# Token columns sent to TensorE as even places, then odd places, and put back in order by the evacuations

## The chip, the cores and the metric

The kernel runs on one core of a Trainium2 chip, in one launch. The metric is the device time of that launch in microseconds, as the median of several runs; 1412.37 us before the change. The engines of the core are TensorE (PE, with its weight loads shown as PEld), VectorE (DVE), ScalarE (ACT), GpSimd (POOL) and SyncE (SP), each with a queue of its own.

## The reference

One inference step of a hybrid decoder layer (one layer, model width 2048) for 256 prompt tokens and 8 sample tokens, all in fp32. Cut to its core:

```python
xn = rms_norm(x, g_mix)
z  = xn @ w_in                       # 2048 -> 3584: pool u, lru x, lru gelu gate, conformer a and b
y_pool = (pool_mixer(u_pool) ...) @ w_pool_br          # 512 -> 2048
y_lru  = (rg_lru(causal_dwconv(u_lru)) * gelu(u_gel)) @ w_lru_br      # 1024 -> 2048
y_conf = silu(layer_norm(causal_dwconv(c_a * sigmoid(c_b)))) @ w_conf_br   # 512 -> 2048
g_a, g_b, g_c = split(sigmoid(xn @ w_gate + b_gate), 3)               # 2048 -> 3 x 2048
x = x + (g_a * y_pool + g_b * y_lru + g_c * y_conf) @ w_out
x = x + square(relu(rms_norm(x, g_mlp) @ w_up)) @ w_down              # 2048 -> 8192 -> 2048
y = rms_norm(x, g_final)             # and the new states of the three mixers
```

## The kernel before

All activations lie with channels on the 128 partitions and the 264 tokens (256 prompt, 8 sample) side by side in the free dimension, 1056 bytes of each partition per tile of 128 channels. A dense layer is then a row of matmuls whose stationary operand is a 128 x 128 block of weights and whose moving operand is one such tile with its 264 columns; the sum over the input channels grows in a PSUM bank (`acc`, eight of them, one 2 KiB bank each).

To keep fp32 precision at the speed of the rounded type `float32r`, weights and activations are each split into a high part (the rounded value) and a low part (the rest). A *split product* is three matmuls, high by high, high by low and low by high (`mm3`, L150 to L153). The very first four products are written out in another order with the same three terms (`first_mm`, L826).

The weights come from HBM in chunks of 128 x 1024, in an order laid down by `weight_plan`. A chunk holds 2 x 4 blocks, that is 8 split products or 24 matmuls. `split` (L147 and L148) rounds a chunk on ACT into `whi` and takes the rest on DVE into `wlo`; both rings have four places, and the split runs three chunks ahead of its use (`AHEAD`). Four banks are filled side by side by the chunks of one group: 8 chunks for a layer with 2048 input channels, 4 for `w_lru_br`, 2 for `w_pool_br` and `w_conf_br`.

After the last chunk of a group each of its four banks is read once, by an evacuation: `lru_x_copy`, `lru_x_evac`, `gel_evac`, `cb_evac`, `ca_evac`, `pool_evac` (the columns of `w_in`), `gate_evac` (L675), `branch_evac` (L688), `out_evac` (L714), `up_evac` (L748), `down_evac` (L764), all on DVE, and on ACT the sigmoids of the small block-diagonal products (`lru_gate_mm`, L404 and L405) and the scale of the pooling products (`grp_mm`, L650). Those that feed a convolution write the prompt columns and the eight sample columns apart. Three all-ones products for the norms (L222, L549, L907) take plain fp32 tiles and do not go through `mm3`.

The order of every engine's queue is written out by the program: work beside the dense stream (convolutions, scans, norms, splits of activations) stands in three queues (`stage`, `run_bg`) or is put off by so many chunks (`later`), with a budget for each engine and chunk. At about 435 us the last evacuations of the LRU branch (L688) are followed on POOL by four additions (L691) and two sums (L542, L543), after which an all-ones product of the conformer's norm (L549) stands in TensorE's queue. At the end, the last `down_evac` is followed by the final norm and the writing of y.

Of the kernel before, what the change touches and what calls it, by code (L numbers as in the profile page):

```python
# [11 lines left out]
AF = mybir.ActivationFunctionType  # L12
ALU = mybir.AluOpType
AX = mybir.AxisListType

P = 128
D = 2048
TP = 256
TS = 8
N = TP + TS  # L20
# [57 lines left out]
def hybrid_step(ctx: ExitStack, tc: tile.TileContext, x_in, par_in, st_in, wall, y_out, st_out):  # L78
    nc = tc.nc
# [4 lines left out]
    def f(ap):  # L84
        return ap.bitcast(F32)
# [7 lines left out]
    X = GX[:, KD:].rearrange("p (k n) -> p k n", k=KD)  # L93
# [6 lines left out]
    rstd = cpool.tile([P, N], F32, name="rstd")  # L100
# [5 lines left out]
    def pv(name, i=None, n=1):  # L106
        a, b = PCOL[name]
        return par[:, a:b] if i is None else par[:, a + i:a + i + n]
# [5 lines left out]
    pext = qtmp[:, 2900:2900 + 4 * (15 + TP)].rearrange("p (g n) -> p g n", g=4)  # L114
    vext = B[3].rearrange("p a n -> p (a n)")[:, 8 * N - 4 * (30 + TP):].rearrange("p (g n) -> p g n", g=4)
# [24 lines left out]
    def split(j, half=None):  # L140
# [6 lines left out]
        nc.scalar.copy(h[:, s], r[:, s])  # L147
        nc.vector.tensor_tensor(lo[:, s], r[:, s], f(h[:, s]), op=ALU.subtract)  # L148

    def mm3(ps, whi_t, wlo_t, xh, xl, first, last):  # L150
        nc.tensor.matmul(ps[:, :N], whi_t, xh, start=first, stop=False)  # L151
        nc.tensor.matmul(ps[:, :N], whi_t, xl, start=False, stop=False)  # L152
        nc.tensor.matmul(ps[:, :N], wlo_t, xh, start=False, stop=last)  # L153
# [47 lines left out]
    def spend(**kw):  # L201
        for e, c in kw.items():
            credit[e] -= c
# [48 lines left out]
    el = B[0].rearrange("p a n -> p (a n)")[:, :8 * (TP + 3)].rearrange("p (a n) -> p a n", a=8)  # L252
# [55 lines left out]
    st_lc = st[:, S_LC:S_LC + 256].rearrange("p (c b k) -> p c b k", c=8, b=8)  # L308
    st_cc = st[:, S_CC:S_CC + 992].rearrange("p (c b k) -> p c b k", c=4, b=8)
    st_po = st[:, S_POOL:S_POOL + 512].rearrange("p (c b k) -> p c b k", c=4, b=8)  # L310
# [3 lines left out]
    TM, GEL, RA, _ = B  # L314
# [10 lines left out]
        return slice(2 * c, 2 * c + 2)  # L325

    def lru_x_copy(ct, ps):
        nc.vector.tensor_copy(CT[:, ct, :], ps[:, :N])
        spend(dve=0.42)

    def lru_x_scale():
# [3 lines left out]
        lru_conv(range(4))  # L335

    def lru_x_evac(ct, ps):
        nc.vector.tensor_tensor(el[:, ct, 3:], ps[:, :TP], rstd[:, :TP], op=ALU.mult)
        nc.vector.tensor_tensor(st_lc[:, ct, :, 3], ps[:, TP:N], rstd[:, TP:], op=ALU.mult)
        spend(dve=0.5)  # L340

    def lru_conv(cts):
# [52 lines left out]
    def lru_gate_mm(ct, c, j):  # L395
        assert "xc" in done
        hi, lo = whi[:, c % NHI, :], wlo[:, c % NHI, :]
        out = []
        for t in range(2):
            s = slice((2 * j + t) * P, (2 * j + t + 1) * P)  # L400
            ps = acc()
            mm3(ps, hi[:, s], lo[:, s], L[:, ct, :], L[:, 8 + ct, :], True, True)
            out.append(ps)
        nc.scalar.activation(RA[:, ct, :], out[0][:, :N], AF.Sigmoid, bias=pv("b_lru_a", ct))  # L404
        nc.scalar.activation(TM[:, ct, :], out[1][:, :N], AF.Sigmoid, bias=pv("b_lru_x", ct))  # L405
        spend(act=1.0)
        if ct % 2:
            def times():
                nc.vector.tensor_tensor(XC[:, ct - 1:ct + 1, :], XC[:, ct - 1:ct + 1, :], TM[:, ct - 1:ct + 1, :],
                                        op=ALU.mult)  # L410
                spend(dve=0.71)

            later(1, times)
# [57 lines left out]

    def gel_evac(ct, ps):
        assert "conv" in done
        nc.vector.tensor_tensor(GEL[:, ct, :], ps[:, :N], rstd, op=ALU.mult)
        spend(dve=0.4)

    def gelu(c0):
# [16 lines left out]
    CT = G[:, 12:16, :]  # L494
    SG = G[:, 16:20, :]
    VC = G[:, 20:24, :]

    def cb_evac(ct, ps):
        nc.vector.tensor_tensor(SG[:, ct, :], ps[:, :N], rstd, op=ALU.mult)
        spend(dve=0.43)  # L500
        if ct == 3:
            later(1, lambda: nc.scalar.activation(SG, SG, AF.Sigmoid))
            later(2, scaled)
# [3 lines left out]
        spend(dve=1.25)  # L507

    def ca_evac(ct, ps):
        nc.vector.tensor_tensor(vext[:, ct, 30:], ps[:, :TP], SG[:, ct, :TP], op=ALU.mult)  # L510
        nc.vector.tensor_tensor(st_cc[:, ct, :, 30], ps[:, TP:N], SG[:, ct, TP:], op=ALU.mult)
        spend(dve=0.5)

    def conf():
# [79 lines left out]


    def pool_evac(gi, ps):
        nc.vector.tensor_tensor(pext[:, gi, 15:], ps[:, :TP], rstd[:, :TP], op=ALU.mult)
        nc.vector.tensor_tensor(st_po[:, gi, :, 15], ps[:, TP:N], rstd[:, TP:], op=ALU.mult)
        spend(dve=0.5)

    Sa = qtmp[:, 0:4 * W].rearrange("p (g n) -> p g n", g=4)
# [1 line left out]
    DU = G[:, 8:12, :]  # L603
# [39 lines left out]
    def grp_mm(c):  # L643
        assert "pool" in done
        hi, lo = whi[:, c % NHI, :], wlo[:, c % NHI, :]
        for gi in range(4):
            s = slice(gi * P, (gi + 1) * P)
            ps = acc()
            mm3(ps, hi[:, s], lo[:, s], Q(gi), Q(8 + gi), True, True)
            nc.scalar.activation(DU[:, gi, :], ps[:, :N], AF.Copy, scale=pv("pool_scale", gi))  # L650
        stage_split("pool", 2, lambda c: Q(slice(2 * c, 2 * c + 2)), lambda c: Q(slice(8 + 2 * c, 10 + 2 * c)), lambda c: DU[:, 2 * c:2 * c + 2, :])
        mark("pool", "grp")

# [18 lines left out]
    def gate_evac(br, g, m, ps):  # L672
        assert {"b_term", "grp"} <= done and (br != 1 or g % 2 == 0 or "lru" in done) and ("conf" in done or br < 2 or g < 3)
        t = gate_tile(br, g, m)
        nc.vector.tensor_tensor(t, ps[:, :N], rstd, op=ALU.mult)  # L675

        def rest():
            nc.scalar.activation(t, t, AF.Sigmoid, bias=pv("b_gate", br * 16 + g * 4 + m))
            spend(act=0.5)

        spend(dve=0.43)
        later(1 + m // 2, rest)

    def branch_evac(br, g, m, ps):
        assert "grp" in done and (br < 1 or "lru" in done) and (br < 2 or "conf" in done)
        t = gate_tile(br, g, m)
        k = g * 4 + m
        nc.vector.tensor_tensor(t, ps[:, :N], t, op=ALU.mult)  # L688
        spend(dve=0.43)
        if br == 1:  # L690
            nc.gpsimd.tensor_tensor(partial(k), t, gate_tile(0, g, m), op=ALU.add)  # L691
            spend(pool=0.8)
        if br == 2:
            nc.gpsimd.tensor_tensor(t, t, partial(k), op=ALU.add)
            spend(pool=0.8)
            later_split(A[:, k, :], A[:, 16 + k, :], t, 1)
# [14 lines left out]
    sq2 = G[:, 20, :]  # L711

    def out_evac(m, ps):
        nc.vector.tensor_tensor(X[:, m, :], X[:, m, :], ps[:, :N], op=ALU.add)  # L714
        spend(dve=0.4)

        hi, lo = bpart(m)

        def one():
            nc.scalar.activation(hi, X[:, m, :], AF.Copy, scale=pv("g_mlp", m))  # L720
            square_add(m)
            spend(act=0.8)

        def other():
            nc.vector.scalar_tensor_tensor(lo, X[:, m, :], pv("g_mlp", m), f(hi),
                                           op0=ALU.mult, op1=ALU.subtract)
            spend(dve=0.35)

        later(m % 4 // 2, one)
        later(m % 4 // 2 + 1, other)  # L730
        if m == KD - 1:
            later(4, lambda: rms_close(sq2))
# [12 lines left out]
    def up_evac(q, m, ps):  # L745
        hi, lo = hid(q, m)
        t = G[:, m % 8, :]
        nc.vector.scalar_tensor_tensor(t, ps[:, :N], 0.0, rstd, op0=ALU.max, op1=ALU.mult)  # L748
        spend(dve=0.4)

        def one():
            nc.scalar.activation(t, t, AF.Square)
            nc.scalar.copy(hi, t)
            spend(act=0.8)

        def other():
            nc.vector.tensor_tensor(lo, t, f(hi), op=ALU.subtract)
            spend(dve=0.35)

        later(1 + m % 4 // 2, one)  # L760
        later(2 + m % 4 // 2, other)

    def down_evac(q, m, ps):
        nc.vector.tensor_tensor(X[:, m, :], X[:, m, :], ps[:, :N], op=ALU.add)  # L764
        spend(dve=0.4)
        if q == 3:
            def rest():
                square_add(m, m < KD - 2)
                nc.scalar.activation(X[:, m, :], X[:, m, :], AF.Copy, scale=gfin[:, m:m + 1])

            later(0 if m >= KD - 4 else 1 + m % 4 // 2, rest)
# [50 lines left out]
    def first_mm(rhs, pss):  # L822
        xh, xl = rhs(0)
        for w, x, start in ((whi, xh, True), (whi, xl, False), (wlo, xh, False)):
            for m in range(4):
                nc.tensor.matmul(pss[m][:, :N], w[:, 0, m * P:(m + 1) * P], x, start=start, stop=False)  # L826

    def tile_mm(i, c, kt, m, rhs, pss, stop):
        s = slice(kt * 512 + m * P, kt * 512 + (m + 1) * P)
# [16 lines left out]
    pss = None  # L846
    for i, ch in enumerate(chunks):
# [13 lines left out]
        kind, gi, c, _ = ch  # L861
        if kind == "dense":
            rhs, fn = group(gi)
            n = groups[gi][2] // 2
            if c == 0:
                pss = [acc() for _ in range(4)]
# [38 lines left out]
    ps = acc()  # L905
# [3 lines left out]
    t = G[:, 9, :]  # L909
# [104 lines left out]
```

## Time and profile before

| what | value |
|---|---|
| median of 3 runs | 1412.37 us (1411.13 to 1413.04) |
| span of the profiled execution, first to last instruction | 1410.3 us |
| granted TensorE clock over the span | 0.997 |
| busy: PE, PEld | 1396.0 us, 1394.3 us (99%) |
| busy: DVE, ACT, POOL | 830.4, 718.7, 98.0 us (59%, 51%, 7%) |
| DMA | 256.95 MB, mean 182 GB/s |

The page gives the profiled execution's own time as its span alone; what the metric counts around the span is the difference to the runs. Busy time of PE counts a matmul from its start to its modelled end, several at once being in flight, so the mean of one (285 ns) is longer than the distance from one to the next. Rows of groups read: line, engine, operation, output<-inputs, shape, count, then busy time and mean of one, then the idle time before them and what ended it.

### The profile page before, as it was taken

How to read it: one execution, taken by the hardware profiler on the slowest of the kernel's cores; microseconds unless marked ns; L12 is line 12 of the kernel's file. 1: busy time of each engine (PE TensorE's matmuls, PEld its weight loads, DVE VectorE, ACT ScalarE, POOL GpSimd, SP SyncE). 2: the span in 40 equal slices, each digit the busy share in tenths (PEclk: the TensorE clock that was granted, in tenths of full speed). 3: DMA queues.
4: the chain of work that ended last, by engine and by line, in shares of the span. 5: the costliest groups of instructions: out<-in, count | busy, mean ns of one | idle time of the engine just before them, and what ended most of it. 6: DMA issues, size and time to landing. Idle time of an engine off the chain costs nothing.

```text
span 1410.3 us, 26593 instructions
## 1 busy us (share of the span) xinstructions
PE 1396.0 (99%) x11418; PEld 1394.3 (99%) x11418; DVE 830.4 (59%) x1031; ACT 718.7 (51%) x1005; POOL 98.0 (7%) x122
## 2 busy tenths in 40 slices
PE   9999999999999999999999999999999999999996
PEld 9999999999999999999999999999999999999996
DVE  7685787776766648565545445544455544455443
ACT  7657576656664645454544334543344533354543
POOL 0230010110102103010000000000000000000012
PEclk9999999999999999999999999999999999999998
DMA  9455555555655554555555555555555555555551
GB/s 335 161 187 187 167 199 183 179 181 181 211 179 177 176 182 153 207 181 179 181 180 180 182 183 181 182 183 180 182 181 182 184 181 181 180 180 180 180 180 62
DMA packets 39286, 256.95 MB, mean 182 GB/s; under 512 B 4352, under 2 KB 5760, under 8 KB 9728
## 3 DMA queue, kind: packets, MB, share of 16 engines
q1 hardware_dynamic: 37872, 253.12, 52.9%
q8 instruction: 89, 1.46, 0.4%
q10 hardware_dynamic: 1152, 1.09, 0.2%
q0 software_dynamic: 144, 1.04, 0.2%
q14 instruction: 29, 0.24, 0.1%
HBM read 252.03 MB, written 3.21 MB: 181 GB/s over the span
## 4 chain that ended last, share of the span: by engine, by line
PE 98%; POOL 0%; DVE 0%; DMA 0%; ACT 0%; issue 0%; DVEq 0%; ACTq 0%
PE acc L153 33%; PE acc L151 33%; PE acc L152 32%; DMA raw<-wall_dram 0%; POOL tmp L691 0%; DVE GX L918 0%; PE acc L826 0%; ACT whi L147 0%; POOL G L543 0%; POOL G L542 0%; DVE wlo L148 0%; PE acc L549 0%; PE acc L222 0%; PE acc L907 0%; DVEq L993 0%
## 5 line engine op out<-in xcount | busy, mean ns | idle before, releaser
L148 DVE TENSOR_TENSOR wlo<-raw,whi 128x1024 fp32r<-128x1024 f32 (+1 forms) x480 | 586.8, 1224 | 551.4 <-ACT whi L147 549.8
L147 ACT CAST whi<-raw 128x1024 fp32r<-128x1024 f32 (+1 forms) x480 | 497.6, 1038 | 629.4 <-PE acc L152 576.1
L151 PE MATMUL acc<-A,whi 128*128 128x264 f32 x1980 | 564.7, 285 | 0.0
L153 PE MATMUL acc<-A,wlo 128*128 128x264 f32 x1980 | 563.4, 285 | 0.0
L152 PE MATMUL acc<-A,whi 128*128 128x264 f32 x1980 | 562.5, 284 | 0.0
L152 PEld LDWEIGHTS acc<-A,whi 128*128 128x128 f32 x1980 | 374.3, 189 | 0.1
L151 PEld LDWEIGHTS acc<-A,whi 128*128 128x128 f32 x1980 | 373.5, 189 | 0.1
L153 PEld LDWEIGHTS acc<-A,wlo 128*128 128x128 f32 x1980 | 373.5, 189 | 0.0
L151 PE MATMUL acc<-xn,whi 128*128 128x264 f32 x1024 | 291.9, 285 | 0.0
L153 PE MATMUL acc<-xn,wlo 128*128 128x264 f32 x1024 | 291.3, 285 | 0.0
L152 PE MATMUL acc<-xn,whi 128*128 128x264 f32 x1024 | 290.8, 284 | 0.0
L152 PEld LDWEIGHTS acc<-xn,whi 128*128 128x128 f32 x1024 | 193.5, 189 | 0.0
L153 PEld LDWEIGHTS acc<-xn,wlo 128*128 128x128 f32 x1024 | 193.1, 189 | 0.0
L151 PEld LDWEIGHTS acc<-xn,whi 128*128 128x128 f32 x1024 | 193.0, 189 | 0.0
L152 PE MATMUL acc<-Q,whi 128*128 128x264 f32 x644 | 182.6, 284 | 0.0
L153 PE MATMUL acc<-LH,wlo 128*128 128x264 f32 x640 | 182.3, 285 | 0.0
L151 PE MATMUL acc<-LH,whi 128*128 128x264 f32 x640 | 182.0, 284 | 0.0
L152 PEld LDWEIGHTS acc<-Q,whi 128*128 128x128 f32 x644 | 121.5, 189 | 0.0
L153 PEld LDWEIGHTS acc<-LH,wlo 128*128 128x128 f32 x640 | 120.4, 188 | 0.0
L151 PEld LDWEIGHTS acc<-LH,whi 128*128 128x128 f32 x640 | 120.4, 188 | 0.0
L738 POOL TENSOR_TENSOR G<-G 128x264 f32<-128x264 f32 x28 | 25.7, 918 | 809.9 <-ACT G L736 808.9
L524 ACT ACTIVATE G<-tmp,par 128x256 f32<-128x256 f32 x120 | 54.3, 500 | 1.7 <-DVE G L527 1.0
(171 smaller groups left out, 762.8 us busy)
## 6 DMA issues: line engine op xcount, KB each, us to landing
raw<-wall_dram SPq DMA_DIRECT2D x230, 1024.0 KB, 4.9
raw<-wall_dram SPq DMA_DIRECT2D x10, 512.0 KB, 5.5
raw<-wall_dram SPq DMA_DIRECT2D x9, 256.0 KB, 3.8
GX<-x_dram SPq DMA_DIRECT2D x6, 264.0 KB, 6.3
so_dram<-st POOLq DMA_DIRECT2D x1, 1018.0 KB, 5.7
st<-st_dram SPq DMA_DIRECT2D x1, 912.0 KB, 8.3
y_dram<-GX SPq DMA_DIRECT2D x2, 396.0 KB, 3.2
y_dram<-GX ACTq DMA_DIRECT2D x4, 132.0 KB, 2.6
```

The source lines that it names most:

```text
L147: nc.scalar.copy(h[:, s], r[:, s])
L148: nc.vector.tensor_tensor(lo[:, s], r[:, s], f(h[:, s]), op=ALU.subtract)
L151: nc.tensor.matmul(ps[:, :N], whi_t, xh, start=first, stop=False)
L152: nc.tensor.matmul(ps[:, :N], whi_t, xl, start=False, stop=False)
L153: nc.tensor.matmul(ps[:, :N], wlo_t, xh, start=False, stop=last)
L524: nc.scalar.activation(dst[:, ct, :TP], vext[:, ct, k:k + TP], AF.Copy, scale=par[:, w:w + 1])
L738: nc.gpsimd.tensor_tensor(sq2, sq2, t, op=ALU.add)
```

## The change

The moving operand of every split product is no longer read as 264 neighbouring columns but as an access pattern of two halves: columns 0, 2, ..., 262 and then 1, 3, ..., 263 (`every_second`). The matmul writes its 264 results side by side as before, so a bank now holds the even tokens in its columns 0 to 131 and the odd ones in 132 to 263. Each evacuation reads the bank back in token order (`res`: column j, then column 132 + j) and names its other operands and its output in pairs of neighbours (`pairs`), so that all have the same shape; everything behind the evacuations is as before. Tiles in SBUF, weights, DMAs and the order of the program are untouched.

```diff
+    def every_second(x):
+        return x.rearrange("p (j t) -> p t j", t=2)
+    def pairs(x):
+        return x.rearrange("p (j t) -> p j t", t=2)
+    def res(ps, a=0, b=N):
+        return ps[:, :N].rearrange("p (t j) -> p j t", t=2)[:, a // 2:b // 2, :]
     def mm3(ps, whi_t, wlo_t, xh, xl, first, last):
+        xh, xl = every_second(xh), every_second(xl)
         nc.tensor.matmul(ps[:, :N], whi_t, xh, start=first, stop=False)
...
     def lru_x_copy(ct, ps):
-        nc.vector.tensor_copy(CT[:, ct, :], ps[:, :N])
+        nc.vector.tensor_copy(pairs(CT[:, ct, :]), res(ps))
...
     def lru_x_evac(ct, ps):
-        nc.vector.tensor_tensor(el[:, ct, 3:], ps[:, :TP], rstd[:, :TP], op=ALU.mult)
-        nc.vector.tensor_tensor(st_lc[:, ct, :, 3], ps[:, TP:N], rstd[:, TP:], op=ALU.mult)
+        nc.vector.tensor_tensor(pairs(el[:, ct, 3:]), res(ps, 0, TP), pairs(rstd[:, :TP]), op=ALU.mult)
+        nc.vector.tensor_tensor(pairs(st_lc[:, ct, :, 3]), res(ps, TP), pairs(rstd[:, TP:]), op=ALU.mult)
...
-        nc.scalar.activation(RA[:, ct, :], out[0][:, :N], AF.Sigmoid, bias=pv("b_lru_a", ct))
+        nc.scalar.activation(pairs(RA[:, ct, :]), res(out[0]), AF.Sigmoid, bias=pv("b_lru_a", ct))
...
-        nc.vector.scalar_tensor_tensor(t, ps[:, :N], 0.0, rstd, op0=ALU.max, op1=ALU.mult)
+        nc.vector.scalar_tensor_tensor(pairs(t), res(ps), 0.0, pairs(rstd), op0=ALU.max, op1=ALU.mult)
...
     def down_evac(q, m, ps):
-        nc.vector.tensor_tensor(X[:, m, :], X[:, m, :], ps[:, :N], op=ALU.add)
+        nc.vector.tensor_tensor(pairs(X[:, m, :]), pairs(X[:, m, :]), res(ps), op=ALU.add)
...
     def first_mm(rhs, pss):
-                nc.tensor.matmul(pss[m][:, :N], w[:, 0, m * P:(m + 1) * P], x, start=start, stop=False)
+                nc.tensor.matmul(pss[m][:, :N], w[:, 0, m * P:(m + 1) * P], every_second(x), start=start, stop=False)
```

The other evacuations (`gel_evac`, `cb_evac`, `ca_evac`, `pool_evac`, `gate_evac`, `branch_evac`, `out_evac`, the second sigmoid and the scale in `grp_mm`) are changed in the same way.

More of the change, by code (lines that the diff above doesn't have):

```diff
@@ L403, in lru_gate_mm @@
             out.append(ps)
-        nc.scalar.activation(RA[:, ct, :], out[0][:, :N], AF.Sigmoid, bias=pv("b_lru_a", ct))
-        nc.scalar.activation(TM[:, ct, :], out[1][:, :N], AF.Sigmoid, bias=pv("b_lru_x", ct))
+        nc.scalar.activation(pairs(RA[:, ct, :]), res(out[0]), AF.Sigmoid, bias=pv("b_lru_a", ct))
+        nc.scalar.activation(pairs(TM[:, ct, :]), res(out[1]), AF.Sigmoid, bias=pv("b_lru_x", ct))
         spend(act=1.0)
@@ L473, in gel_evac @@
         assert "conv" in done
-        nc.vector.tensor_tensor(GEL[:, ct, :], ps[:, :N], rstd, op=ALU.mult)
+        nc.vector.tensor_tensor(pairs(GEL[:, ct, :]), res(ps), pairs(rstd), op=ALU.mult)
         spend(dve=0.4)
@@ L498, in cb_evac @@
     def cb_evac(ct, ps):
-        nc.vector.tensor_tensor(SG[:, ct, :], ps[:, :N], rstd, op=ALU.mult)
+        nc.vector.tensor_tensor(pairs(SG[:, ct, :]), res(ps), pairs(rstd), op=ALU.mult)
         spend(dve=0.43)
@@ L509, in ca_evac @@
     def ca_evac(ct, ps):
-        nc.vector.tensor_tensor(vext[:, ct, 30:], ps[:, :TP], SG[:, ct, :TP], op=ALU.mult)
-        nc.vector.tensor_tensor(st_cc[:, ct, :, 30], ps[:, TP:N], SG[:, ct, TP:], op=ALU.mult)
+        nc.vector.tensor_tensor(pairs(vext[:, ct, 30:]), res(ps, 0, TP), pairs(SG[:, ct, :TP]), op=ALU.mult)
+        nc.vector.tensor_tensor(pairs(st_cc[:, ct, :, 30]), res(ps, TP), pairs(SG[:, ct, TP:]), op=ALU.mult)
         spend(dve=0.5)
@@ L596, in pool_evac @@
     def pool_evac(gi, ps):
-        nc.vector.tensor_tensor(pext[:, gi, 15:], ps[:, :TP], rstd[:, :TP], op=ALU.mult)
-        nc.vector.tensor_tensor(st_po[:, gi, :, 15], ps[:, TP:N], rstd[:, TP:], op=ALU.mult)
+        nc.vector.tensor_tensor(pairs(pext[:, gi, 15:]), res(ps, 0, TP), pairs(rstd[:, :TP]), op=ALU.mult)
+        nc.vector.tensor_tensor(pairs(st_po[:, gi, :, 15]), res(ps, TP), pairs(rstd[:, TP:]), op=ALU.mult)
         spend(dve=0.5)
@@ L649, in grp_mm @@
             mm3(ps, hi[:, s], lo[:, s], Q(gi), Q(8 + gi), True, True)
-            nc.scalar.activation(DU[:, gi, :], ps[:, :N], AF.Copy, scale=pv("pool_scale", gi))
+            nc.scalar.activation(pairs(DU[:, gi, :]), res(ps), AF.Copy, scale=pv("pool_scale", gi))
         stage_split("pool", 2, lambda c: Q(slice(2 * c, 2 * c + 2)), lambda c: Q(slice(8 + 2 * c, 10 + 2 * c)), lambda c: DU[:, 2 * c:2 * c + 2, :])
@@ L674, in gate_evac @@
         t = gate_tile(br, g, m)
-        nc.vector.tensor_tensor(t, ps[:, :N], rstd, op=ALU.mult)
+        nc.vector.tensor_tensor(pairs(t), res(ps), pairs(rstd), op=ALU.mult)
         def rest():
@@ L687, in branch_evac @@
         k = g * 4 + m
-        nc.vector.tensor_tensor(t, ps[:, :N], t, op=ALU.mult)
+        nc.vector.tensor_tensor(pairs(t), res(ps), pairs(t), op=ALU.mult)
         spend(dve=0.43)
@@ L763, in down_evac @@
     def down_evac(q, m, ps):
-        nc.vector.tensor_tensor(X[:, m, :], X[:, m, :], ps[:, :N], op=ALU.add)
+        nc.vector.tensor_tensor(pairs(X[:, m, :]), pairs(X[:, m, :]), res(ps), op=ALU.add)
         spend(dve=0.4)
```

## The prediction

> **What bounds the kernel now.** I read the page first: the shares of the engines, the slices, the chain that ended last.
>
> ```profile
> span 1410.3 us, 26593 instructions
> PE 1396.0 (99%) x11418; PEld 1394.3 (99%) x11418; DVE 830.4 (59%) x1031; ACT 718.7 (51%) x1005; POOL 98.0 (7%) x122
> PEclk9999999999999999999999999999999999999998
> PE 98%; POOL 0%; DVE 0%; DMA 0%; ACT 0%; issue 0%; DVEq 0%; ACTq 0%
> PE acc L153 33%; PE acc L151 33%; PE acc L152 32%; DMA raw<-wall_dram 0%; POOL tmp L691 0%; DVE GX L918 0%; PE acc L826 0%; ACT whi L147 0%; POOL G L543 0%; POOL G L542 0%; DVE wlo L148 0%; PE acc L549 0%; PE acc L222 0%; PE acc L907 0%; DVEq L993 0%
> L151 PE MATMUL acc<-A,whi 128*128 128x264 f32 x1980 | 564.7, 285 | 0.0
> ```
>
> TensorE is the kernel: the chain is PE for 98%, and nearly all of it lies in the three matmuls of `mm3`, which follow each other without idle time at the full granted clock. A matmul's 285 ns is its latency, several being in flight; what counts is the pitch. The busy time of each engine by stretch gives it, and beside it how full DVE is:
>
> ```profile
> 200.00:300.00 100.00, 100.00 (x824) 100.00 (x824) 74.78 (x90) 68.23 (x110) 4.86 (x4) 1.00 0.55 187
> 800.00:900.00 100.00, 100.00 (x824) 100.00 (x823) 49.85 (x58) 41.69 (x51) 0.00 (x0) 1.00 0.55 182
> ```
>
> The columns are span, PE, PEld, DVE, ACT, POOL, then clock and DMA. 824 matmuls in 100 us are 121.4 ns each, alike where DVE is 75% busy and where it is 50%: what sets the pitch lies between TensorE and its operands, and the other engines' traffic does not move it. The page counts 11418 matmul records, of which 30 belong to the all-ones products at L248, L222, L549 and L907; 11388 are split products, and 11388 x 121.4 ns = 1382.5 us. One nanosecond more on the pitch is 11.4 us, or 0.8%. So the question is almost wholly whether a matmul that reads every second column costs the same.
>
> **The moving operand.** Each of the 11388 matmuls reads its 264 columns as 132 at a step of 8 bytes and then the 132 between them; it still writes 264 neighbouring columns of PSUM, only in another order. No instruction is added on any engine, none changes place in its queue, and the weights are loaded as before. No matmul of the trace reads with a step, so the cost is bounded from rows that show what else a pitch can be. The chain near the start, and around the first all-ones product:
>
> ```profile
> 8.62 0.22 PE acc L151
> 8.84 0.22 PE acc L152
> 9.06 0.22 PE acc L153
> 42.45 0.12 PE acc L153
> 42.58 0.45 PE acc L222 x2
> ```
>
> Before the clock is up, a split product takes 220 ns, which is 264 columns at half the later clock and nothing more. At full clock the columns alone would be 220 / 2 = 110 ns, and the pitch is 121.4. So 11.4 ns per matmul belong to something that did not halve with the array clock: the weight load of the next matmul, the issue, or the fetching of the moving operand; the trace does not tell which. An all-ones product in plain fp32 is two instructions in 0.45 us, 225 ns each: a column taken at half pace.
>
> This gives the ends. Upper end: the stepped read comes at half pace, the pitch is L222's 225 ns, and the price is 103.6 ns x 11388 = 1180 us. Lower end: below nothing, if the 11.4 ns come from neighbouring columns being fetched together and the step frees them; at most 11.4 x 11388 = 130 us. Between: nothing, if the stepped read keeps one column per clock, and if a few clocks of bubble at the seam between the halves disappear in the 11.4 ns. I take nothing, because the nearest rows are the 220 ns ones: there the fetch follows the array clock exactly, so at that rate it has no cost of its own, and because the pitch ignores the load that other engines put on the memory, which speaks for a fetch with room to spare.
>
> [...]
>
> **The evacuations.** Each reads its bank back as column j, column 132 + j, and so on, a jump of 528 bytes one way at every element, and writes in token order. Rows of the groups that hold this cost today, and the nearest ones with short runs or steps:
>
> ```profile
> L764 DVE TENSOR_TENSOR GX<-GX,acc 128x264 f32<-128x264 f32 x64 | 23.3, 422 | 8.2 <-PE acc L153 8.2
> L748 DVE SCALAR_TENSOR_TENSOR G<-acc,rstd 128x264 f32<-128x264 f32 x64 | 23.1, 423 | 0.0
> L481 DVE TENSOR_TENSOR tmp<-tmp,tmp 128x528 f32<-128x528 f32 x12 | 7.9, 701 | 0.0
> L333 DVE TENSOR_TENSOR st<-G,rstd 128x32 f32<-128x32 f32 x1 | 0.2, 217 | 0.0
> L634 DVE TENSOR_REDUCE G<-st 128x8 f32<-128x32 f32 x1 | 0.2, 181 | 0.0
> L634 DVE TENSOR_REDUCE G<-st 128x8 f32<-128x16 f32 x1 | 0.2, 164 | 0.0
> L405 ACT ACTIVATE tmp<-acc,par 128x264 f32<-128x264 f32 x8 | 3.8, 479 | 0.0
> ```
>
> Doubling the columns from 264 to 528 adds 701 - 422 = 279 ns. L634 reads runs of two (16 elements) and four (32) out of rows 64 bytes apart, and 16 more elements cost 17 ns, the same 1.06 ns each: short runs alone cost nothing. L333 writes 32 elements one by one 16 bytes apart and takes 217 ns against 181: 36 / 32 = 1.1 ns more per element. So an evacuation costs between 0 and 264 x 1.1 = 297 ns more (a gain is excluded: no element is saved). I take the upper end, since these reads have no runs at all, as L333's writes.
>
> There are 268 full evacuations on DVE (L328, L474, L499, L675, L688, L714, L748, L764, and the long parts of L338, L510, L597) and 20 on ACT: at most 80 us of DVE and 6 of ACT, over the whole span. What hides it: DVE's idle time and the lead of the weight split.
>
> ```profile
> 200.00:300.00 100.00, 10.11 (x28) 1.00 0.55 187
> sum 1397.00, DVE 98.60; mean DVE 7.04
> 800.54 1.05 ACT L147 CAST whi<-raw 128x1024 fp32r<-128x1024 f32 x1 [1.87 <-PE acc L152]
> 801.62 1.23 DVE L148 TENSOR_TENSOR wlo<-raw,whi 128x1024 fp32r<-128x1024 f32 x1 [1.69 <-ACT whi L147]
> 803.45 1.05 ACT L147 CAST whi<-raw 128x1024 fp32r<-128x1024 f32 x1 [1.86 <-PE acc L152]
> ACT whi L147 <- PE acc L152: 576.1, 358, 3.8
> ```
>
> The first two are DVE's work on `acc` alone by stretch (28 instructions between 200 and 300 us, 98.6 us in all): there DVE goes from 74.8 to at most 74.8 + 28 x 0.3 = 83.2 us of 100. The others show the lead: the cast waits until PE has let go of the buffer, and the low half is done at 802.85, 2.3 us later; a chunk is 24 matmuls, 2.9 us, and this split is for the chunk three ahead, so PE reads it some 6.4 us after it is ready. A round of four slower evacuations delays DVE by 1.2 us. A bank is not missed either: the next group accumulates in the other four of eight for at least two chunks, 5.8 us, against four evacuations of 0.72 = 2.9 us. So these 80 us cost nothing on the path, save in two places, where PE waits or has ended:
>
> ```profile
> 435.15 0.35 DVE tmp L688
> 435.59 3.88 POOL tmp L691 x4
> 440.84 1.61 POOL G L543
> PE acc L549 <- POOL G L543: 0.8, 1, 0.8
> 1397.02 0.44 DVE GX L764
> 1397.54 0.43 ACT G L736
> ```
>
> At 435 the first of four evacuations starts POOL's four additions, behind which stands the sum for which PE waits 0.8 us; POOL is slower than DVE, so only one evacuation shows: 0.3 us. The last L764 stands alone behind the last matmul: 0.3 us.
>
> **Sum.** 1410.3 + 0 + 0.3 + 0.3 = 1410.9 us of span. The page gives only a span; the median of the runs, 1412.37, lies 2.1 us above it, for what stands around it, so 1413.0 us.
>
> **The rivals.** *The moving read has a price of its own (slower).* The 11.4 ns by which the pitch exceeds the array time are the fetch of the operand, whose memory does not speed up with the array; the stepped read sweeps 2112 bytes per matmul in place of 1056, and pays them twice. The pitch goes to 132.8 ns, 130 us in all: 1542 us. It decides as soon as the price passes 0.25 ns per matmul, 2.8 us in all. For it: the excess is real and constant. Against it: the weight load, unchanged, would show the same excess. *The read comes at half pace (slower).* Pitch 225 ns, 1412.4 + 1180 = 2592 us; DVE and ACT then idle more. For it: the swept bytes double. Against it: 264 columns in 220 ns, and 110 at full clock, show no limit near. *The step frees the fetch (faster).* The excess goes, 1412.4 - 130 = 1282 us; only the unknown origin of the 11.4 ns speaks for it. *The evacuations do reach the path.* They are late where their bursts meet the wide additions of the convolutions, before 450 us, and three to five rounds of four show with their 1.2 us each: 1412.4 + 3.6 to 6.0, 1416 to 1418 us. That the change does nothing can be left out: the step cannot be merged away, and the order of instructions on each engine stays.
>
> **How the numbers follow.** No change of the pitch 0.56 (of this 0.44 within 0.2%, 0.11 above through the evacuations, 0.01 below), the priced read 0.25, half pace 0.14, faster 0.05. A measurement of this kernel can tell about 0.2% from no change, 2.8 us. Faster 0.06, same 0.44, slower 0.50. Forecast 1413 us, the likeliest case, whose own range is 1410 to 1418. The range goes from 1410 to 1545 and takes in the priced read; half pace (0.14) and the gains (0.06) are left out.
>
> **What would show it.** Right: still 824 matmuls per 100 us, L764 and L748 between 422 and 720 ns, no new wait of PE on L147 or L148, PE idle before L549 up by 0.3 us at most. The priced read: about 753 matmuls per 100 us, with DVE and ACT less busy per stretch. Half pace: about 444. The forecast falls if the pitch moves at all, or if PE waits for DVE in the first 450 us.

## The result and the profile after

The changed kernel takes 2704.22 us (median of 4, 2704.12 to 2704.57) against 1411.85 us for the kernel before on the same chip: 1.915 times as long (95% interval 1.913 to 1.918). The forecast was 1413 us, with a range up to 1545; the case that came, half pace, had been given 0.14 and 2592 us. The page of the changed kernel, its span, engines and chain:

```profile
span 2702.8 us, 26609 instructions
PE 2688.5 (99%) x11418; PEld 2368.7 (88%) x11418; DVE 850.9 (31%) x1031; ACT 721.6 (27%) x1005; POOL 87.2 (3%) x122
PEclk9999999999999999999999999999999999999999
PE 99%; DVE 0%; DMA 0%; ACT 0%; DVEq 0%; issue 0%; ACTq 0%
PE acc L163 33%; PE acc L165 33%; PE acc L164 33%; DMA raw<-wall_dram 0%; PE acc L838 0%; DVE GX L930 0%; PE acc L561 0%; PE acc L234 0%; PE acc L919 0%; ACT whi L147 0%; DVEq L1005 0%; ACT rstd L221 0%; DVE acc L925 0%; DVE G L923 0%; DVE G L922 0%
L163 PE MATMUL acc<-A,whi 128*128 128x264 f32 x1980 | 828.4, 418 | 0.0
```

The counts are the same (11418 matmuls, 1031 and 1005 instructions on DVE and ACT), and DVE and ACT are busy as long as before within 21 us; only their shares have halved. TensorE waits for nobody after its start: these two are its only waits, and the 0.8 us before the conformer's sum is gone, the sum now being early.

```profile
PE acc L260 <- DVE eps L256: 1.1, 1, 1.1
PE acc L838 <- ACT whi L147: 1.0, 1, 1.0
```

What changed is the distance from one matmul to the next. Busy time by stretch of the changed kernel:

```profile
800.00:900.00 100.00, 100.00 (x427) 88.21 (x426) 34.93 (x41) 28.67 (x37) 7.98 (x8) 1.00 0.28 95
2400.00:2500.00 100.00, 100.00 (x427) 88.08 (x426) 28.27 (x34) 24.71 (x34) 0.00 (x0) 1.00 0.27 92
```

427 matmuls in 100 us where there were 824: the pitch, the distance from one matmul's start to the next, went from 121.4 to 234.2 ns. The 11388 matmuls of the split products (three to each product) times 112.8 ns are 1285 us, of the 1292.5 us by which the span grew. The evacuations did nearly nothing:

```profile
L776 DVE TENSOR_TENSOR GX<-GX,acc 128x264 f32<-128x264 f32 x64 | 27.5, 429 | 53.8 <-PE acc L165 53.8
L760 DVE SCALAR_TENSOR_TENSOR G<-acc,rstd 128x264 f32<-128x264 f32 x64 | 27.7, 433 | 36.7 <-PE acc L165 36.7
```

### The profile page after: what moved, and what is told of

The parts are those of the page before. It is cut to its first block, busy times and chain, and to the rows that moved or that the text cites. A ratio compares the mean times of both kernels' runs of the same rounds, so it can differ in the third digit from the quotient of the medians.

```text
span 2702.8 us, 26609 instructions
## 1 busy us (share of the span) xinstructions
PE 2688.5 (99%) x11418; PEld 2368.7 (88%) x11418; DVE 850.9 (31%) x1031; ACT 721.6 (27%) x1005; POOL 87.2 (3%) x122
## 4 chain that ended last, share of the span: by engine, by line
PE 99%; DVE 0%; DMA 0%; ACT 0%; DVEq 0%; issue 0%; ACTq 0%
PE acc L163 33%; PE acc L165 33%; PE acc L164 33%; DMA raw<-wall_dram 0%; PE acc L838 0%; DVE GX L930 0%; PE acc L561 0%; PE acc L234 0%; PE acc L919 0%; ACT whi L147 0%; DVEq L1005 0%; ACT rstd L221 0%; DVE acc L925 0%; DVE G L923 0%; DVE G L922 0%
## 5 line engine op out<-in xcount | busy, mean ns | idle before, releaser
L163 PE MATMUL acc<-A,whi 128*128 128x264 f32 x1980 | 828.4, 418 | 0.0
L165 PE MATMUL acc<-A,wlo 128*128 128x264 f32 x1980 | 827.9, 418 | 0.0
L164 PE MATMUL acc<-A,whi 128*128 128x264 f32 x1980 | 827.7, 418 | 0.0
L164 PEld LDWEIGHTS acc<-A,whi 128*128 128x128 f32 x1980 | 410.7, 207 | 55.4
L163 PEld LDWEIGHTS acc<-A,whi 128*128 128x128 f32 x1980 | 410.8, 207 | 55.2
L163 PE MATMUL acc<-xn,whi 128*128 128x264 f32 x1024 | 429.6, 420 | 0.0
L165 PE MATMUL acc<-xn,wlo 128*128 128x264 f32 x1024 | 429.5, 419 | 0.0
L164 PE MATMUL acc<-xn,whi 128*128 128x264 f32 x1024 | 429.4, 419 | 0.0
L164 PE MATMUL acc<-Q,whi 128*128 128x264 f32 x644 | 267.4, 415 | 0.0
L163 PE MATMUL acc<-LH,whi 128*128 128x264 f32 x640 | 265.6, 415 | 0.0
L165 PE MATMUL acc<-LH,wlo 128*128 128x264 f32 x640 | 265.6, 415 | 0.0
L164 PEld LDWEIGHTS acc<-xn,whi 128*128 128x128 f32 x1024 | 212.4, 207 | 28.6
L163 PEld LDWEIGHTS acc<-xn,whi 128*128 128x128 f32 x1024 | 212.5, 207 | 28.5
L165 PE MATMUL acc<-Q,wlo 128*128 128x264 f32 x132 | 55.0, 417 | 0.0
```

## The experiments

`evac_only` changes the reading back alone; the two whole kernels at the end change both sides; every other kernel changes what is sent to TensorE and leaves the evacuations plain, so that its tokens come out in another order or some terms are left out. The pitch is 100 us divided by the matmuls between 800 and 900 us or, where a tenth of a nanosecond matters, 121.4 ns plus the difference of the spans divided by 11388. Edits are shown in part: where `mm3` takes all its columns in a new order, `first_mm` does too.

**The reading back alone** (`evac_only`): the changed kernel without its two uses of `every_second`.

```diff
     def mm3(ps, whi_t, wlo_t, xh, xl, first, last):
-        xh, xl = every_second(xh), every_second(xl)
```

> Only the reading back is changed (the tokens come out in a wrong order): matmuls read their 264 columns side by side as before, the evacuations read column j, then 132 + j. In the changed kernel L776 and L760 took 429 and 433 ns against 422 and 423. If the evacuations cost nothing on the path, the pitch stays at 824 matmuls per 100 us and the time is 1412 us within 1 us; the prediction's upper price of 297 ns each would show as 720 ns and 0.6 us. If the reading back disturbed TensorE's writes, the time would be above 1415 us.

1411.87 us against 1411.19, ratio 1.0005 (0.9995 to 1.0014). The evacuations by `down_evac`:

```profile
L775 DVE TENSOR_TENSOR GX<-GX,acc 128x264 f32<-128x264 f32 x64 | 23.3, 422 | 8.2 <-PE acc L164 8.2
```

422 ns, exactly as before: a read of PSUM that jumps 528 bytes at every element cost DVE nothing here. The 429 ns of the changed kernel are not the pattern's either: a kernel below with plain evacuations and the same slow pitch (`runs2`) has 429 too. So the whole loss is the moving operand's.

**Where the pace breaks** (`runs66`, `runs4`, `runs2`): the moving operand in runs of r neighbours, the even runs first and then the odd ones.

```diff
+    def cols(x):
+        return x.rearrange("p (a t j) -> p t a j", t=2, j=r)      # r = 66, 4, 2
     def mm3(ps, whi_t, wlo_t, xh, xl, first, last):
+        xh, xl = cols(xh), cols(xl)
```

> Only the moving operand is changed (tokens in a wrong order): the 264 columns go as four runs of 66 neighbours, in the order 1, 3, 2, 4. Pairs theory (TensorE fetches two neighbouring 4-byte columns at once, and a column without its neighbour costs a fetch of its own): 132 fetches as before, 121 ns pitch, 1412 us. Lines theory (the cost goes by 16-byte lines opened, 66 before and 132 in the changed kernel): 66 or 68 lines, 121 to 125 ns, 1412 to 1455 us. Pattern theory (any read that is not one run goes at half pace): 234 ns, about 2704 us.

> Only the moving operand is changed (tokens in a wrong order): runs of 4 neighbours, 16 bytes, every second run first and then the others. Pairs theory: 132 fetches, 121 ns, 1412 us. Lines theory: 66 lines, each opened once, 121 ns, 1412 us, though the sweep is 2112 bytes. Pattern theory: 234 ns, about 2704 us. If the swept bytes were what costs, also 234 ns.

> Only the moving operand is changed (tokens in a wrong order): runs of 2 neighbours, 8 bytes, every second pair first and then the others. Every 16-byte line is opened twice, 132 in all, as in the changed kernel, but each opening takes a pair of neighbours. Pairs theory: 121 ns pitch, 1412 us. Lines theory: 234 ns, about 2704 us. Pattern theory: 234 ns, about 2704 us.

In this order 1451.95, 1406.2 and 2703.67 us (one run each; the kernel before had a median of 1411.19 beside them). Busy time by stretch, `runs66`, `runs4`, `runs2`:

```profile
800.00:900.00 100.00, 100.00 (x801) 100.00 (x801) 48.08 (x54) 37.62 (x41) 0.00 (x0) 1.00 0.51 174
```

```profile
800.00:900.00 100.00, 100.00 (x827) 100.00 (x826) 49.84 (x58) 42.49 (x51) 0.00 (x0) 1.00 0.53 181
```

```profile
800.00:900.00 100.00, 100.00 (x428) 88.20 (x427) 34.64 (x41) 28.57 (x37) 7.98 (x8) 1.00 0.28 95
```

A cut pattern is not slow in itself: 66 runs of four go at full pace, 827 matmuls in 100 us against 824. So the seam, the swept bytes (2112 in `runs4`, as in the changed kernel) and the pattern theory are out. Pairs of neighbours are as slow as single columns, 428 in 100 us against 427, which ends the pairs theory. The lines theory, a price for each 16-byte line opened ("line" counts four neighbouring columns from a tile's start), had all three right, `runs66` even within the stated size; the next run tests it.

**A step of 16 bytes** (`step4`):

```diff
+    def cols(x):
+        return x.rearrange("p (j t) -> p t j", t=4)
```

> Only the moving operand is changed (tokens in a wrong order): columns 0, 4, 8, ... first, then 1, 5, ..., then 2, 6, ..., then 3, 7, ...: a step of 16 bytes, so that every column opens a 16-byte line of its own, 264 in place of 66. Lines theory (a fixed time per line opened, 1.71 to 1.78 ns by the step from 66 lines, 121.4 ns, to 132 lines, 234.4 ns): 460 to 469 ns pitch, about 5270 to 5370 us. Two-pace theory (a line read in full goes at one column per clock, any other at half that): 234 ns, about 2704 us.

2756.41 us, a span of 2754.6:

```profile
800.00:900.00 100.00, 100.00 (x419) 86.83 (x418) 34.41 (x40) 26.32 (x36) 7.94 (x8) 1.00 0.25 85
```

Twice as many lines opened as with a step of 8 bytes cost 4.5 ns more, not the 226 to 235 that the theory asked for. The lines theory fell too. A count that fits the changed kernel and these four runs: a column outside a whole line of four costs about 0.89 ns (234.2 / 264), and the columns of whole lines go about twice as fast (121.4 / 264, 0.46 ns). `runs66` has 8 such columns, because 66 is 16 fours and a half.

**A mixture, and a shifted run** (`runs6`, `shift2`): the first as above with r = 6, the second

```diff
+    def cols(x):
+        return x[:, 2:]
...
-        nc.tensor.matmul(ps[:, :N], whi_t, xl, start=False, stop=False)
-        nc.tensor.matmul(ps[:, :N], wlo_t, xh, start=False, stop=last)
+        nc.tensor.matmul(ps[:, 2:N], whi_t, cols(xl), start=False, stop=False)
+        nc.tensor.matmul(ps[:, 2:N], wlo_t, cols(xh), start=False, stop=last)
```

> Only the moving operand is changed (tokens in a wrong order): runs of 6 neighbours, 24 bytes, the even runs first and then the odd ones; each run is one whole 16-byte line and half of another. Leftover theory (a line taken in full goes at the array's 4 / 264 of 110 ns, 1.67 ns; a column outside of such a four costs 0.89 ns, as in the runs with steps and pairs): 44 x 1.67 + 88 x 0.89 = 152 ns, with the 11 ns by which the run of four times 66 exceeds its own sum 163 ns, about 1885 us. All-or-nothing theory (the pattern as a whole is fast when its innermost run holds at least four columns): 121 to 125 ns, 1412 to 1455 us; or slow because 6 is no multiple of four: 234 ns, 2704 us.

> Two of the three matmuls of every split product outside the first four take 262 neighbouring columns from column 2 on, so that they start in the middle of a 16-byte line; the terms of columns 0 and 1 are left out of them. Leftover theory with fours counted by lines in memory: 65 whole lines and 2 columns, 121 to 122 ns, 1405 to 1420 us. Fours counted from the start of the pattern, which then lie across two lines each: 233 ns for these two, about 2260 us.

1849.03 and 1412.06 us. `runs6` by stretch:

```profile
800.00:900.00 100.00, 100.00 (x625) 99.94 (x624) 45.11 (x54) 37.54 (x54) 6.63 (x8) 1.00 0.39 135
```

160 ns, between the paces, near the 163 of the leftover theory and far from both ends of all-or-nothing. Above 121.4 ns, the span of `runs66` gives 3.5 ns for 8 leftover columns (0.44 each), that of `runs6` 38.4 for 88 (0.44), the changed kernel 113 for 264 (0.43): close to one straight line. The line is a count that fits, not a mechanism, and the 38.4 ns may hold something else too: further down, orders of whole lines without a single leftover column cost as much. `shift2` shows that a long run may start two columns later at no price (1410.3 us of span, as before), so fours that must start with the pattern are out.

**What sets the 121.4 ns** (`half_near`, `half_step`): two of three matmuls with half the columns.

```diff
-        nc.tensor.matmul(ps[:, :N], whi_t, xl, start=False, stop=False)
+        nc.tensor.matmul(ps[:, :N // 2], whi_t, cols(xl), start=False, stop=False)
...                                                                 # the third matmul likewise
+    def cols(x):
+        return x[:, :N // 2]                                        # half_near
+        return x.rearrange("p (j t) -> p t j", t=2)[:, 0, :]        # half_step
```

> Two of the three matmuls of every split product outside the first four take only the first 132 columns, side by side (33 lines in place of 66); the other terms for columns 132 to 263 are left out. It asks what sets the 121.4 ns of the unchanged read. If the fetch does: these two go at 33 x 1.78 + 4 = 63 ns, and the time is near 970 us. If the weight load or the issue does (alike for 132 columns): they stay near 120 ns, and the time stays near 1400 us; a floor in between shows as the pitch itself.

> As the run with two matmuls of three on 132 neighbouring columns, but these 132 are every second one of the 264 (66 lines). Lines theory: as long as a full contiguous read, 117 to 121 ns, and the time stays near 1410 us, whatever the other run gives. If the number of columns decides: the same time as the other run.

1364.14 and 1407.05 us; by stretch, `half_near` and then `half_step`:

```profile
800.00:900.00 100.00, 100.00 (x871) 100.00 (x870) 54.04 (x65) 46.70 (x61) 0.00 (x0) 1.00 0.56 191
```

```profile
800.00:900.00 100.00, 100.00 (x827) 100.00 (x826) 49.85 (x58) 42.55 (x51) 0.00 (x0) 1.00 0.52 180
```

Halving the columns of two matmuls in three takes the mean pitch only from 121.4 to 114.8 ns: three matmuls take 344 ns in place of 364, and if the full one keeps its 121.4, the halved ones take 111.5 each. So half the columns still took 92% of the pitch; the weight loads and the issue are what the kernels have in common, and whether one of them holds the 111.5 ns no run shows. `half_near` had the clock at 0.50 between 15 and 66 us:

```profile
20.00:60.00 40.00, 40.00 (x187) 0.50 0.48 184
```

There its mean pitch is 214 ns against 114.8, 1.86 times as long at half the granted clock. This stretch is also why the span is only 48 us shorter than that of the kernel before, where 11388 times 6.6 ns would give 75: about 27 us of the 1364.14 are not the pattern's. The 132 stepped columns of `half_step` take 120.7 ns by the same sum, as long as 264 in a row; 132 x 0.89 ns are 117, 3 to 4 ns less.

**The order of whole lines** (`runs4_by3`, `runs4_by33`, `runs4_by6`, `runs4_by11`, `runs4_by22`): the one run of `runs4` was 0.35% faster than the kernel before, so the pattern was run with other steps.

```diff
+    def cols(x):
+        return x.rearrange("p (a t j) -> p t a j", t=t, j=4)      # t = 3, 33, 6, 11, 22
```

> Only the moving operand is changed (tokens in a wrong order): runs of 4 neighbours, every third run first, then the next third, then the last; each step opens a line 48 bytes on. The order with every second run took 121.0 ns against 121.4. If the gain comes from no longer opening neighbouring lines one after the other: the same 1406 us, ratio 0.996. If it comes from the step of two lines itself: 1411 us.

> Only the moving operand is changed (tokens in a wrong order): runs of 4 neighbours, the lines in the order 0, 33, 1, 34, ...: 66 lines, each far from the one before, as 33 short rows of the pattern. If any order without neighbouring lines gains: 1406 us. If the number of rows of the pattern costs (33 in place of 2): above 1412 us.

> Only the moving operand is changed (tokens in a wrong order): runs of 4 neighbours, every sixth line, in 6 rows of 11. By-two took 120.9 ns, by-three 119.0, by-33 128.9 against 121.4 in a row. Odd-step theory (only an odd step over the lines gains): 121 ns, 1407 to 1412 us. Row theory (a step of lines gains some 2.5 to 3 ns whatever it is, each row of the pattern costs some 0.3): 119.5 to 120.5 ns, 1390 to 1402 us.

> As before with every eleventh line, in 11 rows of 6. Odd-step theory: 119 ns, 1385 us. Row theory: 121 to 122 ns, 1407 to 1420 us.

> As before with every 22nd line, in 22 rows of 3. Odd-step theory: 121 ns, 1407 to 1412 us. Row theory: 125 ns, about 1450 us.

By three: 1385.09 us, ratio 0.9813 (0.9798 to 0.9828). By 33: 1496.99 us, 1.0603 (1.0585 to 1.0621). One run each by 6, 11 and 22: 1911.77, 1430.82 and 1771.16 us. The stretch from 800 to 900 us for 3, then 6:

```profile
800.00:900.00 100.00, 100.00 (x840) 100.00 (x839) 52.45 (x63) 45.29 (x59) 0.00 (x0) 1.00 0.55 187
```

```profile
800.00:900.00 100.00, 100.00 (x603) 99.93 (x602) 44.97 (x54) 36.91 (x52) 9.97 (x12) 1.00 0.39 128
```

Neither expected theory holds. Rows do not decide (6 rows are slower than 22 and 33), and of the even steps, 6 and 22 lines cost 44 and 32 ns, far beyond what either theory allowed, while 2 lines gain 0.5. Odd steps by 3 gain 2.4 ns, and by 11 and 33 lose 1.6 and 7.5. What arranges these numbers stays open. They also show that runs of four are not enough: these kernels have no column outside a whole line, and two of them lose 44 and 32 ns, where the mixture `runs6` loses 38.

**Whole kernels with the right order** (`runs4_full`, `by3_full`): the evacuations put the tokens back, `up_evac` in two instructions with t=2 and in three with t=3. With t=3 the twelve evacuations before the convolutions take three instructions too (not shown).

```diff
     def every_second(x):
-        return x.rearrange("p (j t) -> p t j", t=2)
+        return x.rearrange("p (a t j) -> p t a j", t=3, j=4)          # runs4_full: t=2, range(2)
     def pairs(x):
-        return x.rearrange("p (j t) -> p j t", t=2)
+        return x.rearrange("p (a t j) -> p a t j", t=3, j=4)
...
-        nc.vector.scalar_tensor_tensor(pairs(t), res(ps), 0.0, pairs(rstd), op0=ALU.max, op1=ALU.mult)
+        for h in range(3):
+            nc.vector.scalar_tensor_tensor(pairs(t)[:, :, h, :], res(ps)[:, :, h, :], 0.0,
+                                           pairs(rstd)[:, :, h, :], op0=ALU.max, op1=ALU.mult)
```

> A whole kernel with the right token order: the columns go in runs of 4 neighbours, the even runs first and then the odd ones, and the evacuations put them back (up_evac in two instructions of 132 columns, because one cannot hold the pattern). The order with plain evacuations had 827 matmuls per 100 us against 824 and took 1406.2 us against 1411.2. If that gain belongs to the order of the lines and the evacuations stay off the path: 1406 us, ratio 0.9965. If it was the chip or chance: 1412 us. If the 64 added instructions on DVE reach the path: above 1412 us.

> A whole kernel with the right token order: runs of 4 neighbours, every third run first; the evacuations put the tokens back, up_evac in three instructions, the twelve evacuations before the convolutions in three as well. The order with plain evacuations took 1385.1 us. If the 140 added short instructions on DVE stay off the path, as the 64 added ones of the order by two did: 1385 us, ratio 0.981. If they reach it: up to 20 us above.

`runs4_full` takes 1406.13 us, ratio 0.9963 (0.9949 to 0.9976); `by3_full` 1385.57 us, ratio 0.9816 (0.9802 to 0.9829), less than both kernels of this case. Its DVE has 140 more instructions and is busy 8 us longer, and the time is that of the order by three with plain evacuations within 0.5 us, so this is hidden:

```profile
PE 1368.9 (99%) x11418; PEld 1366.5 (99%) x11418; DVE 838.2 (60%) x1171; ACT 718.7 (52%) x1005; POOL 97.9 (7%) x122
L766 DVE SCALAR_TENSOR_TENSOR G<-acc,rstd 128x88 f32<-128x88 f32 x192 | 31.4, 241 | 0.0
```

## Why the prediction was wrong

**What held.** TensorE is the whole of it; the pitch decides; nothing else moved. The evacuations stayed off the path, as forecast. Their price was mis-sized all the same: it was put at the upper end, 297 ns, by the L333 row, and is 0; the lower end, by L634, was right. The 36 ns behind the 297 came from setting a product of two inputs (L333) beside a sum over one (L634), so they need not have been a price of the pattern at all. The two terms of 0.3 us that came of it were nothing.

**The step that failed** is "I take nothing", in the paragraph on the moving operand. It rested on the 220 ns of the first split products: there "the fetch follows the array clock exactly, so at that rate it has no cost of its own". That row could only say that the fetch of whole lines is no slower than 0.83 ns per column; it could not say how the fetch of single columns goes, nor on which clock. The same stretch of the changed kernel says it. The first line is from the kernel before, where the pitch drops from 220 to some 125 ns; the others are the last four matmuls of `first_mm` and what follows them in the changed kernel:

```profile
9.28 0.12 PE acc L151
```

```profile
7.90 1.13 PE L838 MATMUL acc<-A,wlo 128*128 128x264 f32 x4
8.85 0.41 PE L163 MATMUL acc<-A,whi 128*128 128x264 f32 x1
```

```profile
9.03 0.24 PE acc L163
9.27 0.24 PE acc L164
9.51 0.24 PE acc L165
9.74 0.23 PE acc L163
```

From 7.90 to 8.85 us four matmuls start, 238 ns each, and it goes on at 0.24 us. The views of these two kernels count the clock as 1.00 there:

```profile
7.50:8.40 0.90, 0.90 (x6) 1.00 1.12 359
```

But the traces' records of the granted clock begin only at 9.17 us in the kernel before, just ahead of its faster matmuls, and at 9.06 us in the changed one; the 1.00 ahead of that is not a record. So "half the later clock" for the 220 ns, and with it the 110 ns of the columns alone, is the author's estimate: `half_near` and `step4` have records of 0.50, but neither gives the pitch of 264 columns in a row there. `step4` has one of half clock, from 7.47 to 10.88 us:

```profile
7.60:10.80 3.20, 3.20 (x15) 0.50 0.99 353
```

```profile
8.68 0.24 PE acc L155
10.84 0.24 PE acc L155
11.08 0.24 PE acc L156
```

Nine matmuls from 8.68 to 10.84 us take 240 ns each at clock 0.50, and 239 at 1.00 later on. So the stepped columns of `step4` took about 0.91 ns each at both recorded clocks; for the step of 8 bytes there are only the 238 ns ahead of the first record and the 234 behind it.

The second reason, that the pitch ignores the other engines' load and the fetch so must have room, was no reason: in `half_near` the pitch stayed near 112 ns even at half the columns, and how long a fetch may be under that no run shows.

**The rivals.** Half pace came true in its effect, with the price mis-sized: L222's 225 ns against 234.2, that is 1180 us against 1292. Its ground, "the swept bytes double", is wrong: `runs4` sweeps as much and took 1406.2 us against 1411.19. So it came near by a row of another data type, not by its argument. The priced read (11.4 ns twice) fell with it. Its premise, that the 11.4 ns over the estimated 110 are the fetch, stays open: 132 columns in a row left a pitch of 111.5, so the pitch was not simply a time for the columns and a fetch on top; but whole lines by three took 2.4 ns off it, so that much went by the order of the read. The gain that the rival "the step frees the fetch" looked for exists to that extent, in an order that nobody had run. So 0.56 had been given to a case for which no row of the trace spoke, a stepped operand never having been run.

**By the visits of a line.** The changed kernel and `runs2` both take two columns at each visit of a line and go at 234 ns; the orders within 2 ns of the 121.4 (`runs4` 120.9, `runs4_by3` 119.0, `runs4_by11` 123) take all four neighbours of a line in sequence, as do some that are slower (165 by six, 153 by 22). A price for each visit does not size the loss either: `step4` goes to a new line at every column, twice as often as the changed kernel, for 4.5 ns more.

## What to carry to other kernels

When the pitch of matmuls is the kernel, an order of the moving operand that keeps its columns in whole 16-byte lines, four fp32 neighbours at a time, is the first to try: here 8 columns of 264 outside them cost 3.5 ns, and all of them 113. In these runs that was needed and not enough: whole lines by steps of two and three kept the pace (120.9 and 119.0 ns against 121.4), by steps of six and 22 the pitch rose by 36% and 26%. A PSUM read put the order back at no cost in time (`evac_only` 1411.87 us against 1411.19; `by3_full` 1385.57 against the 1385.09 of `runs4_by3`).

A bound on an operation that the trace has never shown is not drawn from the row of its undisturbed form: that row tells what else was slower, not what room is left. And a permutation of whole lines deserves a run of its own: the same kernel went from 1385 to 1912 us by the step alone.

## What the runs showed that was not expected

- A moving fp32 column outside a whole 16-byte line cost 0.43 to 0.44 ns more than one inside, counted over 8, 88 and 264 of them (`runs66`, `runs6`, the changed kernel); the count says nothing of the order of the lines, which has a price too.
- Stepped columns did not follow the granted clock in `step4`: 240 ns per matmul at 0.50 and 239 at 1.00. Columns in a row went at 220 ns ahead of the first record of the clock and at 121.4 after it (the kernel before).
- A step of 16 bytes cost hardly more than one of 8: 239 against 234 ns.
- The pitch changed with the step between whole lines: 121.4 ns in a row, 120.9 by two, 119.0 by three, 165 by six, 123 by eleven, 153 by 22, 129 by 33.
- DVE read PSUM with a jump of 528 bytes at each element in 422 ns for 264 elements (`evac_only`, L775), as in a row (L764).
